# One Trainium2 core, a hybrid decoder layer: the recurrence's block-diagonal gate products on the two halves of the array's rows

## The chip, the core and the metric

The kernel runs as one program on one core of a Trainium2 chip. The metric is the device time of one execution in microseconds, the median of several runs. TensorE (PE) multiplies, ACT and DVE work on vectors of up to 128 partitions, POOL (GpSimd) takes some vector work, and SP issues the transfers.

## The reference, cut to what matters

One decoder layer on 16 meta tokens and 1024 tokens of width 1024 (T = 1040 positions): a norm, one wide projection, three mixers side by side (windowed attention, attention with forgetting, a recurrence), their gated sum, an output projection, then a gated feed-forward part and a last norm. The change is in the third mixer, the recurrence, whose 512 channels stand in 8 blocks of 64:

```python
xb = x.reshape(b, t, LRU_BLOCKS, LRU_BLOCK_DIM)              # 8 blocks of 64 channels
r = sigmoid(einsum('bthi,hij->bthj', xb, w_r) + b_r)         # each block has its own 64x64 weights
gi = sigmoid(einsum('bthi,hij->bthj', xb, w_i) + b_i)
log_a = LRU_C * r * log_sigmoid(lam)
h_t = exp(log_a) * h_{t-1} + sqrt(1 - exp(2 * log_a)) * gi * x
```

## The kernel before

All matmuls are exact to float32 by parts: an operand is split into a high part (hi) and a rest (lo), and a product is three matmuls, hi·hi, hi·lo and lo·hi (`mm3`, line 157, its matmul on line 164). `split` (line 128) makes the parts, the high one with ACT (line 131), the rest with DVE (line 132). PSUM has banks of 128x512 under four names: three `mm`, two `sc`, two `tr`, one `ob`. The order of the instructions on each engine is fixed when the program is built, by a scheduler that goes by readiness and by the order in which they were written; `keep_in_program_order` pins an instruction behind the one written before it on its engine. At run time each engine goes through its list in order.

The layer's stages follow each other: norm and first projections (to about 70 us), the recurrence together with the value projections (about 76 to 211 us on PE), attention together with the remaining projections and the branch gates, the branch sum, output projection, feed-forward. In the second of these, `drive` (line 253) mixes two generators: the main one, `lru_main` (line 569), yields projections, and the side one, `lru_side` (line 558), advances one step for each 3500 ns (`LRU_GAP`) of the main one's matmuls. A `yield None` in the side one is such a step. When the main one has nothing left, the side one runs on without it, and the scheduler may place the next stage's projections (gates, queries, keys) between.

The recurrence takes its 512 channels in four tiles m of 128, so two blocks of 64 stand in one tile, on partitions 0 to 63 and 64 to 127. The gate weights come as one array `w_bd` of 128 x 1024: for each tile and gate a 128x128 matrix with the two 64x64 blocks on its diagonal and zeros elsewhere. `lru` (line 508) does one tile: a width-4 convolution on DVE (lines 517, 519) gives x; `split` gives xh and xl; the second input's activation (lines 525 to 528); then for each of the two gates r and g, and each of the column stretches 0:272, 272:528 and 528:1040, one product of three matmuls into an `sc` bank and one sigmoid on ACT out of it (line 536); then tanh, exp and square root on ACT (lines 540, 541, 544), products, the scan and the output's product on DVE (lines 542, 545, 546, 549, 550), another split, and two transfers to DRAM. The gate's bias is one column of `part`, a tile of all small parameters, loaded from `par` at 19 us.

Of the kernel before, what the change touches and what calls it, by code (L numbers as in the profile page):

```python
# [9 lines left out]
F32 = mybir.dt.float32  # L10
F32R = mybir.dt.float32r
AF = mybir.ActivationFunctionType
# [4 lines left out]
P = 128  # L17
D = 1024
# [18 lines left out]
P_CW, P_CB, P_BR, P_BI, P_LM, P_NF = 0, 16, 20, 24, 28, 32  # L37
# [9 lines left out]
def f32(ap):  # L47
    return ap.bitcast(F32)
# [17 lines left out]
def hybrid_block(ctx, tc, h_in, w_in, w_v0, w_v1, w_bd, par, rows, gains, relt, onehot,  # L66
                 maskrow, cmask, w_br, w_out, w_fi, w_fo, out):
    nc = tc.nc
    act, dve, pool, pe = nc.scalar, nc.vector, nc.gpsimd, nc.tensor

    def dma(dst, src):
        nc.sync.dma_start(f32(dst) if dst.dtype == F32R else dst, f32(src) if src.dtype == F32R else src)

    def pad(pool, n):

        pool.tile([P, n // 4], F32, name=f"pad{uid[0]}")
        uid[0] += 1
# [3 lines left out]
    wp = ctx.enter_context(tc.tile_pool(name="wstream", bufs=2, side="left"))  # L81
# [11 lines left out]
    def nm(s):  # L93
        uid[0] += 1
        return f"{s}_{uid[0]}"

    def bank(tag, bufs, label):
        return pp.tile([P, 512], F32, tag=tag, bufs=bufs, name=nm(tag + label))

    mm_bank = lambda label="": bank("mm", 3, label)  # L100
    sc_bank = lambda label="": bank("sc", 2, label)
    tr_bank = lambda label="": bank("tr", 2, label)
# [25 lines left out]
    def split(hi, lo, src, scale=None, pin=False):  # L128

        if scale is None:  # L130
            a = act.activation(hi, src, AF.Copy)  # L131
            i = dve.tensor_tensor(lo, src, f32(hi), ALU.subtract)  # L132
            if pin:
                tc.keep_in_program_order(i)
        else:
            a = act.activation(hi, src, AF.Copy, scale=scale)
            i = dve.scalar_tensor_tensor(lo, src, scale, f32(hi), ALU.mult, ALU.subtract)
        return a.ins, i.ins

    def load_w(src, n, pl=None, tag="w", bufs=None, lo_on_pool=False):  # L140
        pl = pl or wp
        kw = {} if bufs is None else dict(bufs=bufs)
        if n == D:
            raw = wp.tile([P, n], F32, tag="wr", name=nm("wr"))
        else:
            raw = pl.tile([P, n], F32, tag=tag + "r", name=nm(tag + "r"), **kw)
        dma(raw, src)
        hi = pl.tile([P, n], F32R, tag=tag + "h", name=nm(tag + "h"), **kw)
        lo = pl.tile([P, n], F32R, tag=tag + "l", name=nm(tag + "l"), **kw)
        if lo_on_pool:  # L150
            act.activation(hi, raw, AF.Copy)
            pool.tensor_tensor(lo, raw, f32(hi), ALU.subtract)
        else:
            split(hi, lo, raw)
        return hi, lo

    def mm3(ps, terms, first=True):

        n = 3 * len(terms)
        cost = ps.shape[-1] / 2.4 + 3  # L160
        i = 0
        for ah, al, bh, bl in terms:
            for a, b in ((ah, bh), (ah, bl), (al, bh)):
                pe.matmul(ps, a, b, start=first and i == 0, stop=i == n - 1, skip_group_check=not first)  # L164
                i += 1
            yield 3 * cost

    def run(gen):
        for _ in gen:
            pass  # L170

    def log_sigmoid(dst, z, pl, shape):

        e, s, s2, a = (pl.tile(shape, F32, name=nm("ls")) for _ in range(4))
        dve.scalar_tensor_tensor(e, z, -1.0, z, ALU.mult, ALU.min)
        act.activation(e, e, AF.Exp)
        dve.tensor_scalar(s, e, 2.0, None, ALU.add)
        dve.reciprocal(s, s)
        dve.tensor_tensor(s, s, e, ALU.mult)
        dve.tensor_tensor(s2, s, s, ALU.mult)  # L180
        dve.tensor_scalar(a, s2, 1.0 / 17, 1.0 / 15, ALU.mult, ALU.add)
        for c in (13, 11, 9, 7, 5, 3, 1):
            dve.tensor_tensor(a, a, s2, ALU.mult)
            dve.tensor_scalar(a, a, 1.0 / c, None, ALU.add)
        dve.tensor_tensor(a, a, s, ALU.mult)
        dve.tensor_scalar(s, z, 0.0, None, ALU.min)
        dve.scalar_tensor_tensor(dst, a, -2.0, s, ALU.mult, ALU.add)
# [14 lines left out]
    def rstd_of(x, n, junk):  # L202

        q = cp.tile([P, 2], F32, tag="sq2", bufs=4, name=nm("sq"))
        for i in range(2):
            act.activation(junk[i], x[i], AF.Square, accum_out=q[:n, i:i + 1])
        return rstd_from(q, n)

    def halves(x):
        return x[:, :512], x[:, 512:]  # L210
# [80 lines left out]
    with tc.tile_pool(name="r0", bufs=1, side="right", reuse_waits="tile") as r0:  # L291
# [128 lines left out]
        def products(j, w, chunk):  # L420

            c, off, n, t0 = chunk
            ps = mm_bank(f"_w{j}")
            kinds = {"hh": (w[0], uh[c]), "hl": (w[0], ul[c]), "lh": (w[1], uh[c])}

            def some(kind, ks, first=False, last=False):
                a, b = kinds[kind]
                for k in ks:
                    t_.matmul(ps[:, :n], a[:, k * P:(k + 1) * P], b[:, k, off:off + n],
                              start=first and k == ks[0], stop=last and k == ks[-1])  # L430
            return ps[:, :n], some
# [33 lines left out]
        ps, some = products(YC, wy[0], (0, NM, 256, 0))  # L465
# [39 lines left out]

    r1 = ctx1.enter_context(tc.tile_pool(name="r1", bufs=1, side="right", reuse_waits="tile"))

    def lru(m, bdh, bdl):
        xr, y = lru_in[m]
        pc = lambda b: part[:, b + m:b + m + 1]  # L510
        cw = lambda i: part[:, P_CW + 4 * m + i:P_CW + 4 * m + i + 1]

        def t1(tag, dt=F32):
            return r1.tile([P, T], dt, tag=tag, bufs=1, name=nm(tag))

        x = t1("x")
        dve.tensor_scalar(x, xr[:, 0:T], cw(0), pc(P_CB), ALU.mult, ALU.add)
        for i in range(1, 4):
            dve.scalar_tensor_tensor(x, xr[:, i:i + T], cw(i), x, ALU.mult, ALU.add)
        xh, xl = t1("xh", F32R), t1("xl", F32R)  # L520
        split(xh, xl, x)
        yield None

        th = t1("th")[:, :S]
        act.activation(th, y, AF.Square, scale=math.sqrt(0.044715))
        dve.scalar_tensor_tensor(th, th, 1.0, y, ALU.add, ALU.mult)
        act.activation(th, th, AF.Tanh, scale=math.sqrt(2.0 / math.pi))
        dve.scalar_tensor_tensor(y, th, 1.0, y, ALU.add, ALU.mult)
        yield None
        r, g = t1("r"), t1("g")  # L530
        for dst, gi, b in ((r, 0, P_BR), (g, 1, P_BI)):
            col = slice((2 * m + gi) * P, (2 * m + gi + 1) * P)
            for t0, n in ((0, 272), (272, 256), (528, 512)):
                ps = sc_bank()
                run(mm3(ps[:, :n], [(bdh[:, col], bdl[:, col], xh[:, t0:t0 + n], xl[:, t0:t0 + n])]))
                act.activation(dst[:, t0:t0 + n], ps[:, :n], AF.Sigmoid, bias=pc(b))
                yield None

        w = t1("q")
        act.activation(w, r, AF.Tanh, scale=lsc[:, 0, m:m + 1])  # L540
        act.activation(r, r, AF.Exp, scale=lsc[:, 1, m:m + 1])
        dve.tensor_tensor(g, g, x, ALU.mult)
        yield None
        act.activation(w, w, AF.Sqrt)
        dve.scalar_tensor_tensor(w, r, 1.0, w, ALU.add, ALU.mult)
        dve.tensor_tensor(g, w, g, ALU.mult)
        yield None
        hs = t1("x")
        dve.tensor_tensor_scan(hs, r, g, 0.0, ALU.mult, ALU.add)
        dve.scalar_tensor_tensor(y, hs[:, NM:T], 0.5, y, ALU.mult, ALU.mult)  # L550
        yield None
        ch, cl = t1("xh", F32R), t1("xl", F32R)
        split(ch[:, :S], cl[:, :S], y)
        dma(osp[2, 0, m], ch[:, :S])
        dma(osp[2, 1, m], cl[:, :S])
        yield None

    def lru_side():
        bdh, bdl = load_w(w_bd, D, r1, "bd")
        pad(r1, 448)  # L560

        log_sigmoid(lsc[:, 1], part[:, P_LM:P_LM + 4], r1, [P, 4])
        dve.tensor_scalar(lsc[:, 0], lsc[:, 1], -4.0, None, ALU.mult)
        dve.tensor_scalar(lsc[:, 1], lsc[:, 1], 8.0, None, ALU.mult)
        for m in range(4):
            yield ("lru", m)
            yield from lru(m, bdh, bdl)

    def lru_main():
        done.update({("lru", 0), ("lru", 1)})  # L570
# [450 lines left out]
    with tc.tile_pool(name="r4", bufs=1, side="right", reuse_waits="tile") as r4:  # L1021
        with tc.tile_pool(name="r4b", bufs=1, side="right", reuse_waits="tile") as r4b:
            for c in range(2):
                u2[c] = [pair_tile(mp if c else bp) for k in range(KT // 2)]
                for tt in range(4 * c, 4 * c + 4):
                    ht = r4.tile([P, D], F32, tag="ht", bufs=2, name=nm("ht"))
                    dma(ht, h_in[NM + tt * P:NM + (tt + 1) * P])
                    t0 = (tt - 4 * c) * P
                    q = slice(t0, t0 + P)
                    for half in range(2):  # L1030
                        n = slice(512 * half, 512 * half + 512)
                        ps = mm_bank(f"_wo{tt}")
# [5 lines left out]
                    r = rstd_of(halves(ht), P, halves(xg))  # L1038
# [410 lines left out]
```

## Time and profile before

| | |
|---|---|
| median of 3 runs | 1641.56 us (1641.25 to 1641.89) |
| the profiled execution's own time | 1640.56 us |
| its span, first to last instruction | 1638.8 us |
| PE busy | 1627.0 us, 8189 matmuls |
| ACT, DVE, POOL busy | 760.5, 997.5, 388.3 us |

The profile is of one execution. Engine busy times are a union of the recorded instructions; a matmul's record includes its way through the array, so records of consecutive matmuls overlap, and the time that one costs is read from start to start. PEld are the weight loads of PE, recorded apart.

### The profile page before, as it was taken

How to read it: one execution, taken by the hardware profiler on the slowest of the kernel's cores; microseconds unless marked ns; L12 is line 12 of the kernel's file. 1: busy time of each engine (PE TensorE's matmuls, PEld its weight loads, DVE VectorE, ACT ScalarE, POOL GpSimd, SP SyncE). 2: the span in 40 equal slices, each digit the busy share in tenths (PEclk: the TensorE clock that was granted, in tenths of full speed). 3: DMA queues.
4: the chain of work that ended last, by engine and by line, in shares of the span. 5: the costliest groups of instructions: out<-in, count | busy, mean ns of one | idle time of the engine just before them, and what ended most of it. 6: DMA issues, size and time to landing. Idle time of an engine off the chain costs nothing.

```text
span 1638.8 us, 22729 instructions
## 1 busy us (share of the span) xinstructions
PE 1627.0 (99%) x8189; PEld 1373.6 (84%) x8189; DVE 997.5 (61%) x1817; ACT 760.5 (46%) x1399; POOL 388.3 (24%) x325
## 2 busy tenths in 40 slices
PE   9999999999999999999999999999999999999998
PEld 8898888888888888888888888888888888888886
DVE  6566666555666666642447447967777766466554
ACT  6456465555555555552335334433333333355342
POOL 3000000012122221110055000267756666200000
PEclk9999999999999999999999999999999999999999
DMA  6323342213324142349753322345554453698632
GB/s 224 110 95 104 120 139 97 94 64 123 117 78 123 59 124 82 106 138 332 259 183 116 119 88 76 126 159 181 212 178 148 154 182 114 224 352 277 195 127 103
DMA packets 110738, 241.96 MB, mean 148 GB/s; under 512 B 11929, under 2 KB 23529, under 8 KB 110370
## 3 DMA queue, kind: packets, MB, share of 16 engines
q1 hardware_dynamic: 110482, 239.99, 43.4%
q8 instruction: 64, 1.05, 0.3%
q10 hardware_dynamic: 144, 0.52, 0.1%
q14 instruction: 48, 0.39, 0.1%
HBM read 162.93 MB, written 72.21 MB: 143 GB/s over the span
## 4 chain that ended last, share of the span: by engine, by line
PE 93%; DVE 2%; ACT 2%; DMA 1%; issue 1%; SPq 0%; POOL 0%; DVEq 0%; ACTq 0%; POOLq 0%
PE mm_w L164 26%; PE mm_s L164 13%; PE mm_br L164 8%; PE tr_s L164 7%; PE mm_wo L164 5%; PE mm_x L1313 4%; PE tr_y L1313 4%; PE sc_y L1313 4%; PE mm_v L164 3%; PE sc_s L164 3%; PE ob L711 3%; PE tr L722 3%; PE ob_x L1313 1%; PE mm_g L164 1%; PE mm_u L164 1%; PE sc L796 1%
## 5 line engine op out<-in xcount | busy, mean ns | idle before, releaser
L164 PE MATMUL mm_w<-uh,wh 128*128 128x512 f32 (+2 forms) x744 | 291.5, 392 | 0.0
L164 PE MATMUL mm_w<-uh,wl 128*128 128x512 f32 (+2 forms) x744 | 279.4, 376 | 0.0
L164 PE MATMUL mm_w<-ul,wh 128*128 128x512 f32 (+2 forms) x744 | 279.4, 375 | 0.0
L164 PEld LDWEIGHTS mm_w<-uh,wl 128*128 128x128 f32 x744 | 140.0, 188 | 25.3
L164 PEld LDWEIGHTS mm_w<-uh,wh 128*128 128x128 f32 x744 | 140.4, 189 | 12.5
L164 PEld LDWEIGHTS mm_w<-ul,wh 128*128 128x128 f32 x744 | 140.8, 189 | 11.5
L132 DVE TENSOR_TENSOR ab<-raw,ab 128x1024 fp32r<-128x1024 f32 x77 | 92.8, 1223 | 72.0 <-ACT ab L131 71.5
L131 ACT ACTIVATE ab<-raw 128x1024 fp32r<-128x1024 f32 x77 | 80.8, 1060 | 95.3 <-PE ob_x L1313 23.3
L131 ACT ACTIVATE wh<-wr 128x1024 fp32r<-128x1024 f32 (+1 forms) x84 | 72.0, 859 | 106.8 <-PE mm_w L164 50.5
L164 PE MATMUL mm_br<-o,wh 128*128 128x512 f32 x384 | 118.3, 389 | 0.0
L164 PE MATMUL mm_s<-pt,ar 128*128 128x512 f32 x492 | 118.2, 389 | 0.0
L132 DVE TENSOR_TENSOR pl<-tr,ph 128x384 fp32r<-128x384 f32 (+2 forms) x160 | 87.2, 554 | 47.1 <-ACT ph L131 43.0
L164 PEld LDWEIGHTS mm_s<-pt,ar 128*128 128x128 f32 x492 | 92.3, 188 | 19.2
L132 DVE TENSOR_TENSOR wl<-wr,wh 128x1024 fp32r<-128x1024 f32 x45 | 56.7, 1261 | 72.0 <-ACT wh L131 71.8
L131 ACT ACTIVATE ph<-tr 128x384 fp32r<-128x384 f32 (+2 forms) x160 | 76.9, 486 | 50.3 <-PE tr L722 48.2
L812 POOL TENSOR_SCALAR s<-s,sm 128x144 f32<-128x144 f32 (+3 forms) x64 | 48.6, 761 | 171.8 <-DVE sm L811 143.4
L164 PE MATMUL mm_wo<-wo,hl 128*128 128x512 f32 x384 | 89.2, 391 | 0.0
L164 PEld LDWEIGHTS mm_br<-o,wh 128*128 128x128 f32 x384 | 72.1, 188 | 15.0
L164 PEld LDWEIGHTS mm_wo<-wo,hl 128*128 128x128 f32 x384 | 71.6, 188 | 14.7
L722 PE MATMUL tr<-ident,s 128*128 128x128 f32 x480 | 79.8, 274 | 0.8 <-DVE pl L132 0.2
L164 PE MATMUL mm_br<-o,wl 128*128 128x512 f32 x192 | 74.7, 389 | 0.0
L722 PEld LDWEIGHTS tr<-ident,s 128*128 128x128 f32 x480 | 59.0, 140 | 18.0 <-DVE pl L132 3.9
(315 smaller groups left out, 3580.7 us busy)
## 6 DMA issues: line engine op xcount, KB each, us to landing
wr<-w_in_dram SPq DMA_DIRECT2D x45, 512.0 KB, 3.6
wr<-w_fi_dram SPq DMA_DIRECT2D x44, 512.0 KB, 4.5
raw<-asp SPq DMA_DIRECT2D x77, 256.0 KB, 3.3
asp<-a SPq DMA_DIRECT2D x66, 256.0 KB, 2.8
gz<-z SPq DMA_DIRECT2D x48, 256.0 KB, 2.1
sg<-gz SPq DMA_DIRECT2D x48, 256.0 KB, 2.7
o<-osp SPq DMA_DIRECT2D x24, 512.0 KB, 4.9
fo<-w_fo_dram SPq DMA_DIRECT2D x22, 512.0 KB, 4.4
```

The source lines that it names most:

```text
L131: a = act.activation(hi, src, AF.Copy)
L132: i = dve.tensor_tensor(lo, src, f32(hi), ALU.subtract)
L164: pe.matmul(ps, a, b, start=first and i == 0, stop=i == n - 1, skip_group_check=not first)
L711: pe.matmul(ob[:, q0:q0 + b - a], vt[:, c], x[:, a:b], start=count == 0, stop=count == n_mm - 1, skip_group_check=True)
L722: pe.transpose(tb[:, col:col + P], src, ident)
L796: pe.matmul(sc[:, :n], qs, kh[:, k0:k0 + n], start=True, stop=False)
L812: pool.tensor_scalar(s[:, :nk], s[:, :nk], den, 1.0, ALU.mult, ALU.mult)
L1313: pe.matmul(banks[x], a[:, 0, q], b[:, 1], start=first and j == 0 and c == 0, stop=j == NJ - 1 and c % 3 == 2, skip_group_check=True)
```

## The change

The gate products no longer multiply by a 128x128 matrix with two zero blocks. The weights are rearranged: rows 0 to 63 hold, for each tile, the first block's 64 columns of gate r and then of gate g, rows 64 to 127 the same of the second block, so that the array `bdh` (and `bdl`) is 128 x 512, and a half of it, 64 rows by 128 columns, is both gates of one block. For each column stretch there are two banks, one from `sc` and one from `tr`. Three products (hi·hi, hi·lo, lo·hi) are written, each as a matmul of rows 0 to 63 into the first bank and one of rows 64 to 127 into the second; all but the first of the six are pinned behind the matmul written before. A bank then holds gate r of its block in partitions 0 to 63 and gate g in 64 to 127, so four activations of 64 partitions take the two banks apart. They need their biases by bank partitions: a new tile `bias2` is filled by four small transfers from `par`. The two `split` calls of the weights go over 64 rows each. The padding behind shrinks by as much as `bias2` takes.

```diff
-    def lru(m, bdh, bdl):
+    def lru(m, bdh, bdl, bias2):
...
-        for dst, gi, b in ((r, 0, P_BR), (g, 1, P_BI)):
-            col = slice((2 * m + gi) * P, (2 * m + gi + 1) * P)
-            for t0, n in ((0, 272), (272, 256), (528, 512)):
-                ps = sc_bank()
-                run(mm3(ps[:, :n], [(bdh[:, col], bdl[:, col], xh[:, t0:t0 + n], xl[:, t0:t0 + n])]))
-                act.activation(dst[:, t0:t0 + n], ps[:, :n], AF.Sigmoid, bias=pc(b))
+        for t0, n in ((0, 272), (272, 256), (528, 512)):
+            sl = slice(t0, t0 + n)
+            banks = sc_bank()[:, :n], tr_bank()[:, :n]
+            for i, (a, b) in enumerate(((bdh, xh), (bdh, xl), (bdl, xh))):
+
+                for z, ps in enumerate(banks):
+                    rw = slice(64 * z, 64 * z + 64)
+                    mm = pe.matmul(ps, a[rw, m * P:m * P + P], b[rw, sl], start=i == 0, stop=i == 2)
+                    if i or z:
+                        tc.keep_in_program_order(mm)
+            for z, ps in enumerate(banks):
+                rw = slice(64 * z, 64 * z + 64)
+                for gi, dst in enumerate((r, g)):
+                    src = slice(64 * gi, 64 * gi + 64)
+                    act.activation(dst[rw, sl], ps[src], AF.Sigmoid, bias=bias2[src, z, m:m + 1])
                 yield None
...
-        bdh, bdl = load_w(w_bd, D, r1, "bd")
-        pad(r1, 448)
+        raw = wp.tile([P, D], F32, tag="wr", name=nm("wr"))
+        dma(raw, w_bd)
+        raw = raw.rearrange("p (m g c) -> p m g c", m=4, g=2)
+        bdh, bdl = (r1.tile([P, D], F32R, tag=f"bd{x}", name=nm(f"bd{x}"))[:, :512] for x in "hl")
+
+        bias2 = r1.tile([P, 2, 4], F32, name="bias2")
+        for z in range(2):
+            rw = slice(64 * z, 64 * z + 64)
+            split(*(x[rw].rearrange("p (m g c) -> p m g c", m=4, g=2) for x in (bdh, bdl)), raw[rw, :, :, rw])
+            for gi, b in enumerate((P_BR, P_BI)):
+                dma(bias2[64 * gi:64 * gi + 64, z], par[rw, b:b + 4])
+        pad(r1, 416)
...
-            yield from lru(m, bdh, bdl)
+            yield from lru(m, bdh, bdl, bias2)
```

## Rows read from the trace of the kernel before

**Rows 1.** The page's head: span, busy time of each engine, the granted clock in 40 slices (9 is full speed within a tenth), and the chain of work that ended last, by engine.
```profile
span 1638.8 us, 22729 instructions
PE 1627.0 (99%) x8189; PEld 1373.6 (84%) x8189; DVE 997.5 (61%) x1817; ACT 760.5 (46%) x1399; POOL 388.3 (24%) x325
...
PEclk9999999999999999999999999999999999999999
...
PE 93%; DVE 2%; ACT 2%; DMA 1%; issue 1%; SPq 0%; POOL 0%; DVEq 0%; ACTq 0%; POOLq 0%
```

**Rows 2.** Busy time of each engine in the recurrence's stage (stretch, its length, then PE, PEld, DVE, ACT, POOL with their instructions, the granted clock, the DMA engines' share and GB/s): the whole stretch, 15 us near its end, and the whole stretch for the instructions of the `sc` banks alone.
```profile
75.00:211.00 136.00, 134.81 (x806) 122.31 (x805) 81.06 (x138) 78.61 (x108) 0.00 (x0) 1.00 0.32 111
...
195.00:210.00 15.00, 13.81 (x80) 11.90 (x79) 11.12 (x13) 8.78 (x14) 0.00 (x0) 1.00 0.47 148
...
75.00:211.00 136.00, 15.12 (x72) 11.75 (x72) 0.00 (x0) 12.09 (x24) 1.00 0.32 111
```

**Rows 3.** What PE waited for between 60 and 330 us: engine, tile and line, the releaser, the total in us, how often, the longest.
```profile
PE sc L164 <- ACT xh L131: 1.2, 1, 1.2
```

**Rows 4.** The timeline around one gate product of each column stretch (start and duration in us, engine, line, operation, out<-in, rows*columns of the weights, the moving operand): PE, and for the first group PE's weight loads.
```profile
76.54 0.29 PE L164 MATMUL sc<-xh,bdh 128*128 128x272 f32 x1
76.92 0.39 PE L164 MATMUL mm_w<-uh,wh 128*128 128x512 f32 x1
...
76.55 0.19 PEld L164 LDWEIGHTS sc<-xl,bdh 128*128 128x128 f32 x1
...
81.02 0.28 PE L164 MATMUL sc<-xh,bdh 128*128 128x256 f32 x1
81.38 0.39 PE L164 MATMUL mm_w<-uh,wh 128*128 128x512 f32 x1
...
84.78 0.39 PE L164 MATMUL sc<-xh,bdh 128*128 128x512 f32 x1
85.47 0.39 PE L164 MATMUL mm_w<-uh,wh 128*128 128x512 f32 x1
```

**Rows 5.** The timeline around the one product of 32 rows (two matmuls, merged into one line in the first view; the line that begins at 30.95 is the second of them, from a view that begins there), and the weight load of the 32-row product.
```profile
30.30 0.28 PE L164 MATMUL mm_w<-ul,x1h 128*128 128x256 f32 x1
30.41 0.28 PE L164 MATMUL mm_w<-uh,x1l 128*128 128x256 f32 x1
30.62 0.81 PE L482 MATMUL sc<-oh,rt 32*8 32x383 f32 x2
...
30.62 0.09 PEld L482 LDWEIGHTS sc<-oh,rt 32*8 32x8 f32 x2
...
30.95 0.48 PE L482 MATMUL sc<-oh,rt 32*8 32x383 f32 x1
31.36 0.66 PE L218 MATMUL tr<-ident,xg 128*128 128x128 f32 x4
```

**Rows 6.** The timeline where gate products stand between small transposes whose weights have 8 columns: PE, then one weight load of such a transpose.
```profile
148.26 0.48 PE L164 MATMUL sc<-xh,bdh 128*128 128x512 f32 x1
148.57 0.27 PE L592 MATMUL tr<-ident,lf 128*8 128x128 f32 x1
148.60 0.48 PE L164 MATMUL sc<-xl,bdh 128*128 128x512 f32 x1
...
148.37 0.08 PEld L592 LDWEIGHTS tr<-ident,lf 128*8 128x8 f32 x1
```

**Rows 7.** ACT's groups of instructions by shape, 55 to 235 us: out<-in, shapes, count, busy us, mean ns, idle before.
```profile
L536 ACT ACTIVATE r<-sc,part 128x512 f32<-128x512 f32 x4 | 2.8, 689 | 5.2 <-PE sc L164 5.2
L536 ACT ACTIVATE r<-sc,part 128x272 f32<-128x272 f32 x4 | 2.0, 489 | 0.3 <-PE sc L164 0.3
...
L536 ACT ACTIVATE g<-sc,part 128x256 f32<-128x256 f32 x4 | 1.9, 474 | 0.0
...
L283 ACT ACTIVATE xr<-mm_w 128x512 f32<-128x512 f32 x3 | 1.8, 586 | 4.8 <-PE mm_w L164 4.8
...
L131 ACT ACTIVATE k<-mm_w 64x512 fp32r<-64x512 f32 x2 | 1.2, 594 | 0.1
```

**Rows 8.** The chain of work that ended last, in order of time (start, us, what): its stretch through the recurrence's third tile to the operand of the fourth, and the end of the attention stage.
```profile
181.46 1.05 ACT q L540
...
202.27 1.08 ACT xh L131
...
729.00 42.85 PE mm_w L164 x189
```

**Rows 9.** The timeline where the gate weights are split, and the issues of SP's queue (SPq) beside it: the small parameters' transfer, and the load that follows the split.
```profile
19.14 0.42 SPq L72 DMA_DIRECT2D part<-par_dram  x1
...
55.66 1.05 ACT L131 ACTIVATE bdh<-wr 128x1024 fp32r<-128x1024 f32 x1
...
57.99 0.33 SPq L72 DMA_DIRECT2D wr<-w_in_dram  x1
...
66.29 1.05 ACT L131 ACTIVATE wh<-wr 128x1024 fp32r<-128x1024 f32 x1
```

**Rows 10.** The weight loads of a run of attention products, of which two have only 128 columns.
```profile
706.24 0.19 PEld L711 LDWEIGHTS ob<-pl,v 128*128 128x128 f32 x1
706.35 0.19 PEld L711 LDWEIGHTS ob<-ph,v 128*128 128x128 f32 x1
706.46 0.19 PEld L711 LDWEIGHTS ob<-pl,v 128*128 128x128 f32 x1
```

## The prediction, on record before the changed kernel ran

> **What bounds the kernel now.** I read the page's head first, then the chain that ended last, then the recurrence's stretch alone. TensorE is busy in 1627.0 of 1638.8 us, at a granted clock of full speed (the 2.4 GHz level) in all 40 slices [rows 1]; the chain is 93% PE [rows 1]. So time taken out of TensorE's order of work is time off the end, as long as nothing new makes it wait. The change lies between 76 and 211 us. There TensorE is busy in 134.8 of 136 us and ACT in 78.6; what TensorE lacks lies at 195 to 210 [rows 2]. PE waited for the recurrence once, 1.2 us, for the operand of the last channel tile [rows 3].
>
> **The products' own time.** One gate product is three matmuls. Start to start, from a group's first matmul to the next tile's first, a group of 272 columns takes 76.92 - 76.54 = 0.38 us, one of 256 columns 81.38 - 81.02 = 0.36, one of 512 columns 85.47 - 84.78 = 0.69 [rows 4]. Weight loads begin as the matmul ahead begins, and so are hidden [rows 4]. Four channel tiles with two gates make 8 x (0.38 + 0.36 + 0.69) = 11.4 us of TensorE. That is all the change can touch: 0.7% of the run. (By one row for all 72, the stretch's busy time in these banks is 15.1 us, but a matmul's record reaches over the start of the next [rows 2].)
>
> **Part 1, half the rows, two at a time.** The new loop has as many matmuls and as many columns: per column stretch three products times two halves, against three times two gates. It gains only if the matmul on rows 64 to 127 runs while that on rows 0 to 63 runs. Nothing in this trace has two matmuls on different rows at once, so the bounds are: below, each pair takes the time of one, 4 x 1.43 = 5.7 us in place of 11.4 (a gain of 5.7); above, they run one after the other, 11.4 again. I take the lower figure: the two have no weight, row or bank in common, and the engine does start a matmul of 8 columns and the next of 128 within 0.03 us of each other (148.57 and 148.60) [rows 6].
>
> **Part 2, going into half rows and out again.** The trace has one place where TensorE goes from all rows to a part of them and back, a product of 32 rows at 30.62 us. The matmul ahead begins at 30.41 and, of 256 columns, takes 0.12 as its forerunners do, so it is through at 30.53; the 32-row one begins at 30.62, and its weights are loaded then, not under the matmul ahead: 0.09 us lost [rows 5]. On the way back, the second begins at 30.95, takes 0.33 like the first (30.95 - 30.62), is through at 31.28; the next full one begins at 31.36 with its load: 0.08 lost [rows 5]. A load that is not hidden holds up its own matmul too: the gate products between transposes last 0.48 instead of 0.39 us, 0.09 more [rows 4, 6]. So one visit costs 0.09 + 0.09 + 0.08 + 0.09 = 0.35 us. The new loop makes at most 12 visits (4 tiles x 3 stretches, other work between them): 4.2 us. Bounds: 0, if 64 rows are no change of state for the array as 32 were; 4.2 above. I take 4.2, since these are the only rows with such a step. The Trainium skill (TensorEngine Tiling, Key Properties) says that a change of tiling mode drains the engine; by that rule the sum is the one below, without it the gain would be the whole 5.7 us. The trace agrees for 32 rows, and has no row for 64.
>
> **Part 3, sigmoids.** 24 activations of 128 rows become 48 of 64 rows, with as many columns each. Halving the rows saves nothing: a 64x512 copy takes 594 ns, a 128x512 one 586 [rows 7]. So ACT gets 8 x (0.49 + 0.48 + 0.69) = 13.3 us more [rows 7], over 136 us in which it is busy for 78.6 [rows 2]. For tiles 0 and 1 the main stream's products cover it. For tiles 2 and 3 the products come in a burst and the rest hangs in a chain of ACT and DVE work from 180 to 203 us, at the end of which PE waited [rows 3, 8]; the chain gets about 3.3 us longer per tile. Taken at 0: 42.85 us of one TensorE run, four gate projections with nothing beside them, stand behind the attention stage at 729 us, and such work can be ordered ahead while the recurrence lags [rows 8]. Without that cover it costs up to 2 x 3.3 = 6.6 us.
>
> **Part 4, banks, the split and the small transfers.** The second half takes transpose banks, of which there are two, as of the others; a column stretch now holds its two banks for four activations, some 2 us, and the next stretch has the other two: 0, bounded by one such wait, 2 us. Five of the six matmuls are pinned in their written order, which adds no wait. Splitting the weights on 64 rows twice instead of 1024 columns once: ACT 1.05 us becomes 2 x 0.59 [rows 7, 9], and DVE's part is taken to grow alike. The weight buffer comes free about 0.2 us later for the load that SP issues at 57.99, needed at 66.29 [rows 9]: hidden. Four transfers into the new bias tile join SP's queue; an issue like theirs takes 0.42 us [rows 9], so 1.7 us, and SP has nothing to issue for many us before 57.99. If they were to stand behind a buffer that is late, the load at 57.99 would be late with them, against a slack of some 4 us. Cost 0, above 2 us, nothing to gain.
>
> **The sum.** -11.4 + 5.7 + 4.2 = -1.5 us. The profiled execution took 1640.56 us, of which 1638.8 are the span; it lies 1.0 below the median of the runs, 1641.56. From the median: 1640.1 us, 0.1% down. A measurement here can tell apart about 0.2%, 3.3 us; so the forecast is no difference that shows.
>
> **Rivals.**
> Whole gain: the halves overlap and the visits are nearly free, because 64 rows with loads for each half let the next load run ahead. Then 1641.6 - 5.7 = 1635.9 us, or about 1637 with half of the 0.17 us of a visit's two gaps. For it: at 148.37 the weights of an 8-column transpose are loaded under a full matmul [rows 6]. Against: the 32-row load was not [rows 5].
>
> Weight loads set the pace: loads of 128 columns come no closer than 0.11 us (706.24, 706.35, 706.46) [rows 10], and a pair needs two. In turn, a pair takes 0.22, 0.22 and 0.23 us, 12 x 0.67 = 8.0 with three products and four tiles; -11.4 + 8.0 + 4.2 = +0.8: 1642.4 us. If a half's load also waited for that half's own matmul, a pair would be its columns' time plus 0.11: 12 x (0.125 + 0.12 + 0.23 + 0.33) = 9.7, and the sum is +2.5, 1644.1 us. The Trainium skill (TensorE: Matmul & The Clock Gate, Part 3, The mechanism) has loads overlap running matmuls only where the row groups differ, which is this last case. The trace speaks against the rule: on all rows a load begins at 76.55 beside a matmul of the same rows that began at 76.54 [rows 4].
>
> **Slower:** the change doesn't do what it says, the halves run one after the other. Then the visits are all that is left: +4.2, 1645.8 us, slower by 0.26%. It decides from the first pair: starts of the two halves a full 0.12 or 0.23 us apart. For it: no row of two matmuls running whole side by side; against: nothing that they share.
>
> Late recurrence: the chain of tiles 2 and 3 ends 6.6 us later and TensorE's order has its products too early; -1.5 + 6.6 = +5.1, 1646.7 us. For it: the 1.2 us wait that is there now [rows 3]; against: the spare gate work.
>
> **Chances.** Forecast 0.42, whole gain 0.24, weight loads 0.14, one after the other 0.11, late recurrence 0.09. Faster by over 0.2% (under 1638.3) is the whole gain and the edge of the forecast: 0.25. Slower (over 1644.8) is the last two and an edge of the weight loads: 0.22. Within: 0.53. The range goes from just under the whole gain, 1635.5, to 1645.3, which leaves out the last rival and most of the one before it. The forecast's own range is 1638 to 1642.
>
> **What would show it.** Starts of the halves of a pair within 0.11 us of each other and pairs 0.12 or 0.23 apart: part 1 right. A gap of about 0.09 ahead of the first half-row matmul, its load not under the matmul ahead, and the same on the way out: part 2 right. Pairs 0.22 apart whatever their columns: the weight loads. ACT's busy time up by 13 us with PE's waits for xh unchanged: part 3 right. I am wrong if PE's total falls by 5 us or more, or if PE waits for sigmoids or banks.

## The result and the profile after

The changed kernel took 1649.71 us (median of 6 runs, 1647.54 to 1654.34), the kernel before 1641.71 beside it: ratio 1.005, interval 1.0039 to 1.006. That is 8 us or 0.5% slower, outside the range of the prediction and on the side that had a chance of 0.22. The profiled execution is the quickest of the six, 1647.54 us, with a span of 1645.7 against 1638.8 before: 6.9 us to explain. The three longest runs (1650.7 to 1654.3 us) have a mean granted clock of 0.996, the three shortest 0.998 or 0.999, so the time spent at the lower clock differs between executions of the same program.

The head of the page after: span, busy times, and TensorE's busy tenths in 40 slices.

```profile
span 1645.7 us, 22757 instructions
PE 1629.6 (99%) x8189; PEld 1369.5 (83%) x8189; DVE 1003.7 (61%) x1818; ACT 772.7 (47%) x1422; POOL 390.8 (24%) x325
PE   9999989999999999999999999999999999999998
```

Beside [rows 1] there are as many matmuls, ACT has 12.2 us more, and one slice of TensorE, the sixth (206 to 247 us), shows an 8. What TensorE waited for between 60 and 330 us (releaser, total, times, longest; two waits of 0.3 us are left out):

```profile
PE sc L768 <- DVE sm L770: 2.2, 1, 2.2
PE sc L538 <- ACT g L545: 1.5, 1, 1.5
PE mm_w L164 <- DVE wl L132: 1.2, 1, 1.2
PE sc L538 <- ACT xh L131: 0.8, 1, 0.8
```

Before, there was 1.2 for xh [rows 3]. Now xh has 0.8, and three new waits of over 1 us stand beside it. Busy time by stretch (PE, PEld, DVE, ACT, POOL, the granted clock, DMA share, GB/s): one stretch after, then the sums from 60 to 330 us, after and before:

```profile
180.00:195.00 15.00, 13.74 (x53) 10.51 (x54) 3.17 (x3) 13.33 (x19) 0.00 (x0) 0.89 0.09 37
...
sum 270.00, PE 263.34 PEld 224.42 DVE 165.34 ACT 165.40 POOL 9.88; mean PE 14.63 PEld 12.47 DVE 9.19 ACT 9.19 POOL 0.55
...
sum 270.00, PE 268.06 PEld 234.52 DVE 169.92 ACT 158.45 POOL 9.98; mean PE 14.89 PEld 13.03 DVE 9.44 ACT 8.80 POOL 0.55
```

The 15 us from 180 had a mean clock of 0.89, so 15 x 0.11 = 1.65 us of TensorE's work was lost there. Over 60 to 330 us, TensorE's idle time is 270 - 263.34 = 6.66 us against 1.94 before. Idle 4.7 and clock 1.65 make 6.4 us. The products themselves give back about 1.0 (below), so 7.9 us are to be explained and 1.5 are in neither sum. An idle time begins only where the record of the matmul ahead ends: the wait that shows 1.46 us below is 181.26 - 179.29 = 1.97 us from start to start, less 0.34 for the matmul ahead (0.23, and 0.11 for its load, as below) 1.63. At 0.17 us more for each of six waits, an estimate, that is 1 of the 1.5 us; the last 0.5 stay open.

**The products themselves came out as forecast.** PE at the first gate group (start, duration, line, out<-in, rows*columns of the weights, moving operand), then PE's loads for the second pair:

```profile
76.36 0.39 PE L164 MATMUL mm_w<-uh,wl 128*128 128x512 f32 x1
76.68 0.39 PE L538 MATMUL sc<-xh,bdh 64*128 64x272 f32 x1
76.68 0.39 PE L538 MATMUL tr<-xh,bdh 64*128 64x272 f32 x1
76.91 0.29 PE L538 MATMUL sc<-xl,bdh 64*128 64x272 f32 x1
76.91 0.29 PE L538 MATMUL tr<-xl,bdh 64*128 64x272 f32 x1
77.04 0.28 PE L538 MATMUL sc<-xh,bdl 64*128 64x272 f32 x1
77.04 0.28 PE L538 MATMUL tr<-xh,bdl 64*128 64x272 f32 x1
77.25 0.50 PE L164 MATMUL mm_w<-uh,wh 128*128 128x512 f32 x1
```
```profile
76.79 0.19 PEld L538 LDWEIGHTS sc<-xl,bdh 64*128 64x128 f32 x1
76.79 0.19 PEld L538 LDWEIGHTS tr<-xl,bdh 64*128 64x128 f32 x1
```

Both halves of each pair begin at the same hundredth. From the first pair to the next full matmul it is 77.25 - 76.68 = 0.57 us, with 0.09 ahead of it (76.36, and 0.23 as its like take, to 76.68), and the full matmul behind is 0.11 longer than its like (0.50 against 0.39): 0.77 in all, where two gate groups took 2 x 0.38 [rows 4].

**Where the time went.** ACT at channel tile 2, from the table load ahead of its sigmoids to the tanh and the table load behind that:

```profile
178.93 1.28 ACT L545 ACT_TABLE_LOAD   x1
180.23 0.48 ACT L545 ACTIVATE r<-sc,bias 64x272 f32<-64x272 f32 x1
180.72 0.48 ACT L545 ACTIVATE g<-sc,bias 64x272 f32<-64x272 f32 x1
...
186.99 1.17 ACT L549 ACTIVATE q<-r,lsc 128x1040 f32<-128x1040 f32 x1
188.17 1.28 ACT L550 ACT_TABLE_LOAD   x1
```

and PE beside it:

```profile
179.29 0.51 PE L164 MATMUL mm_w<-uh,wh 128*128 128x512 f32 x1
181.26 0.50 PE L538 MATMUL sc<-xh,bdh 64*128 64x512 f32 x1 [1.46 <-ACT g L545]
...
184.07 0.63 PE L164 MATMUL mm_w<-uh,wl 128*128 128x512 f32 x1
184.50 0.63 PE L164 MATMUL mm_w<-uh,wh 128*128 128x512 f32 x1
...
187.24 0.39 PE L164 MATMUL mm_w<-ul,wh 128*128 128x512 f32 x1
187.47 0.40 PE L164 MATMUL mm_w<-uh,wl 128*128 128x512 f32 x1
```

The two pairs of banks are full, and the third stretch waits until ACT has loaded its table and read the first bank twice. Then matmuls of 512 columns stand 0.43 us apart (184.07, 184.50) where they take 0.23 at 187.24 and 187.47: the 1.2 GHz level, from about 183.5 to 186.9. The tanh begins at 186.99; before, it began at 181.46 by the chain [rows 8]. That compares unlike places: the old order had gate r complete after its own three sigmoids, and two of gate g's stood behind the tanh; now r is complete only with the last stretch. All sigmoids of the tile are done where ACT loads the table behind them; before, its first sigmoids and that load:

```profile
178.85 0.85 ACT L536 ACTIVATE r<-sc,part 128x272 f32<-128x272 f32 x2
...
183.48 1.28 ACT L541 ACT_TABLE_LOAD   x1
```

So the tile is 188.17 - 183.48 = 4.7 us late there. From ACT's first sigmoid (180.23 after, 178.85 before) it is 7.94 against 4.63 us: 3.3 us are the added sigmoids, and the rest is mostly the table load at 178.93, which ACT did not have at that place before.

The end of tile 3 (DVE: the split of x, before and after, and the last product y, before and after; then SP's queue, then DVE in the next stage, after):

```profile
203.37 1.24 DVE L132 TENSOR_TENSOR xl<-x,xh 128x1040 fp32r<-128x1040 f32 x1 [0.74 <-ACT xh L131]
208.38 1.24 DVE L132 TENSOR_TENSOR xl<-x,xh 128x1040 fp32r<-128x1040 f32 x1 [0.72 <-ACT xh L131]
223.54 1.23 DVE L550 SCALAR_TENSOR_TENSOR y<-x,y 128x1024 f32<-128x1024 f32 x1
232.78 1.23 DVE L559 SCALAR_TENSOR_TENSOR y<-x,y 128x1024 f32<-128x1024 f32 x1
233.92 1.22 DVE L132 TENSOR_TENSOR wl<-wr,wh 128x1024 fp32r<-128x1024 f32 x1
...
245.92 0.37 DVE L770 CUSTOM_DVE_ANT_0 s<-sc,nb,nsink 128x144 f32<-128x144 f32 x1 [4.09 <-DMA nb<-bss]
```
```profile
235.12 0.32 SPq L72 DMA_DIRECT2D osp<-xh  x1
...
239.69 0.89 SPq L72 DMA_DIRECT2D nb<-bss  x2
```

DVE splits the next stage's weights (wl) only behind the recurrence's last product y: PE waits 1.2. SP issues the attention's bias `nb` behind the recurrence's last store `osp`: DVE's softmax step waits for it, its bank stays taken, and PE waits 2.2. Both are places in a fixed list behind an instruction that has become late: before, SP issued `osp` at 225.88 and `nb` at 230.55, about as far apart.

### The profile page after: what moved, and what is told of

The parts are those of the page before. It is cut to its first block, busy times and chain, and to the rows that moved or that the text cites. A ratio compares the mean times of both kernels' runs of the same rounds, so it can differ in the third digit from the quotient of the medians.

```text
span 1645.7 us, 22757 instructions
## 1 busy us (share of the span) xinstructions
PE 1629.6 (99%) x8189; PEld 1369.5 (83%) x8189; DVE 1003.7 (61%) x1818; ACT 772.7 (47%) x1422; POOL 390.8 (24%) x325
## 4 chain that ended last, share of the span: by engine, by line
PE 93%; ACT 3%; DVE 2%; DMA 1%; issue 1%; SPq 0%; POOL 0%; DVEq 0%; ACTq 0%; POOLq 0%
PE mm_w L164 25%; PE mm_s L164 13%; PE mm_br L164 8%; PE tr_s L164 7%; PE mm_wo L164 5%; PE mm_x L1333 4%; PE tr_y L1333 4%; PE sc_y L1333 4%; PE ob L731 4%; PE mm_v L164 3%; PE sc_s L164 3%; PE tr L742 3%; PE ob_x L1333 1%; PE mm_g L164 1%; PE mm_u L164 1%; PE sc L816 1%
```

## The experiments

Theories: **A**, the doubled sigmoids lengthen ACT's part of the recurrence's chain, and what stands behind it in the queues is late. **B**, the half-row products and their pairs of banks cost by themselves. **C** (later called **L**), no price but another order: the scheduler places everything differently, and a fixed order meets banks and operands that are not ready. **P**, the pace of the recurrence's steps; **T** and **S** belong to e13, **E** to e14 and e15. Differences below are in us against the kernel before in its own runs; at 1640 us the intervals reach 1.5 to 2.5 us to either side.

**e1.** The kernel before, with each sigmoid in two halves.

```diff
-                act.activation(dst[:, t0:t0 + n], ps[:, :n], AF.Sigmoid, bias=pc(b))
+                for z in range(2):
+                    rw = slice(64 * z, 64 * z + 64)
+                    act.activation(dst[rw, t0:t0 + n], ps[rw, :n], AF.Sigmoid, bias=pc(b)[rw])
```


> The kernel before with its 128x128 products, but each of the 24 sigmoids taken in two halves of 64 rows, so ACT has the changed kernel's 48 sigmoids and PE the old work. Theory A (the loss is ACT's: the doubled sigmoids make tiles 2 and 3 of the recurrence late and hold banks): 4 to 8 us above the kernel before, y of the last tile (DVE, the product after the scan) at about 230 us instead of 223.5, and PE waits for nb or wl near 235 to 245 us. Theory B (the loss is in the half-row products: visits, their clock): within 1 us of the kernel before. Theory C (any edit here that makes the scheduler order the work anew costs this much): a shift of either size, with the waits at other places than in the changed kernel.

1647.54 us, +6.1. The last y begins at 231.24, and PE waits 1.9 for xh and 1.3 for the attention's `sm`. At this pace, the sigmoids alone cost nearly what the change costs.

**e2.** Half-row products, but one sigmoid of 128 rows per bank.

```diff
-                rw = slice(64 * z, 64 * z + 64)
-                for gi, dst in enumerate((r, g)):
-                    src = slice(64 * gi, 64 * gi + 64)
-                    act.activation(dst[rw, sl], ps[src], AF.Sigmoid, bias=bias2[src, z, m:m + 1])
+                act.activation((r, g)[z][:, sl], ps, AF.Sigmoid, bias=bias2[:, z, m:m + 1])
```


> The changed kernel's half-row products, but one sigmoid of 128 rows for each bank (24 in all, as before), written whole into r or g. What is left out: the rearrangement of the gates by block, so r and g hold mixed rows and the output is not the reference's. Theory A: the loss is gone, 1.5 us below the kernel before to 1 us above it, the recurrence's last y at about 222 to 224 us. Theory B: still 6 to 8 us above. Theory C: anything, with waits at new places.

1648.86 us, +7.1, so the products alone also cost nearly the whole: A by itself is not enough, or one order tells little. What PE waited for:

```profile
PE mm_w L164 <- DVE q L673: 5.2, 2, 4.3
PE sc L538 <- ACT r L542: 1.4, 1, 1.4
```

The 5.2 us are evictions of the next stage's queries, which DVE had among the recurrence's last products, up to behind y (219.30 to 227.0 us); stretches at the lower clock follow both waits (180 to 195 us: 1.65 us, 225 to 240: 3.0). The last y begins at 225.08, only 1.5 us late: at this pace most of the loss came without a late end.

**e3.** The third stretch in other banks.

```diff
-            banks = sc_bank()[:, :n], tr_bank()[:, :n]
+            banks = (sc_bank(), tr_bank()) if t0 < 528 else (o_bank(), mm_bank())
+            banks = [x[:, :n] for x in banks]
```


> The changed kernel, with the 512-column stretch's two banks taken from ob and mm instead of sc and tr, so the third stretch need not wait for the sigmoids of the first. Theory A with its bank part: PE's wait of 1.5 us at 181 us and the stretch at the lower clock behind it (1.7 us) go, 2 to 4 us below the changed kernel, so 3 to 6 above the kernel before; the late end of the recurrence and its waits near 235 to 245 us stay. If the bank wait is not a cause: as the changed kernel.

1666.48 us, +25: one wait of 26.1 us at 180. As the kernel reads, the `mm` banks go round in written order, so the next stage's projections had to wait for tile 3's product; no run tests this. The experiment says nothing about bank holding.

**e4 to e8 and e18.** Old and changed kernel at other paces, which give other orders.

```diff
-LRU_GAP = 3500.0
+LRU_GAP = 2500.0   # e4, e18; 3000.0 in e5, e6; 4000.0 in e7, e8
```


> The changed kernel with the recurrence's steps spaced 2500 instead of 3500 ns of main work. Theory A: the recurrence runs further ahead beside the value projections, its last y comes 5 us or more earlier than 232.8, and 3 to 7 us of the loss go (within 4 us of the kernel before). Theory B: as the changed kernel, 6 to 8 us above. Theory C: anything.

> The kernel before with LRU_GAP 3000 in place of 3500: the side generator is advanced every 3000 ns of the main one's matmuls, so the recurrence's work is put earlier among the projections; products and sigmoids as before. Theory L (the change's own price is small; any other order of the work between 178 and 260 us meets banks and operands that are not ready, and the kernel before at 3500 happens to be a well-timed order): slower than before, by 2 to 8 us, with waits of PE of over 1 us in that stretch. Theory A (the added sigmoids themselves make the recurrence late, whatever the order): without the added sigmoids no loss, 1639 to 1643.

> The changed kernel with LRU_GAP 3000. Theory L: its difference to the old products at the same gap lies anywhere from -4 to +4 us. Theory A: +4 to +8 us above the old products at the same gap.

> The kernel before with LRU_GAP 4000: the recurrence's work is put later among the projections. Theory L: slower than before by 2 to 8 us, with waits of PE of over 1 us between 178 and 260 us. Theory A: a later recurrence alone costs some too, but less than the changed kernel loses: 1641 to 1645.

> The changed kernel with LRU_GAP 4000. Theory L: its difference to the old products at the same gap lies anywhere from -4 to +4 us. Theory A: +4 to +10 us above the old products at the same gap, since the recurrence starts later still.

> The kernel before at LRU_GAP 2500, where the changed kernel took 1646.03 us. Theory A: 1639 to 1643, the changed kernel 3 to 7 us above. If the changed kernel's loss were gone at this early pace, 1644 or above.

With e16 and e17 (below), each median with its ratio to the kernel before:

| LRU_GAP | old products | half rows, whole sigmoids | changed |
|---|---|---|---|
| 2500 | 1641.69, 1.0005 | | 1646.03, 1.0029 |
| 3000 | 1643.49, 1.0014 | 1645.64, 1.0024 | 1655.03, 1.0081 |
| 3500 | 1641.71 (the kernel before) | 1648.86, 1.0043 | 1649.71, 1.005 |
| 4000 | 1641.19, 0.9996 | 1642.37, 1.0005 | 1648.74, 1.0041 |

The old products lose 2 us or less at every pace, so another pace alone does not make the loss. L is not out as a part of it: in e14, one more order, the old products lose 5.3 us. The changed kernel stands above them by 3.9, 11.0, 8.2 and 7.4 us (from the differences of the ratios, each good to some 2 to 3 us): the change costs at each of four orders. The size goes with the order: 4 to 11 us. A's ranges were missed three times: e6 is above its 4 to 8 us, e4, 4.8 us above the kernel before, is just over its 4, and e5 is 0.5 us above its 1643.

**e9 and e10.** The change also drops steps of the side generator, from twelve per tile to nine, which the prediction had not counted. e9 gives the changed kernel its six gate steps back, e10 takes three from the kernel before.

```diff
                     act.activation(dst[rw, sl], ps[src], AF.Sigmoid, bias=bias2[src, z, m:m + 1])
-                yield None
+                    if gi:
+                        yield None
```
```diff
                 act.activation(dst[:, t0:t0 + n], ps[:, :n], AF.Sigmoid, bias=pc(b))
-                yield None
+                if (gi, t0) in ((0, 272), (1, 0), (1, 528)):
+                    yield None
```


> The changed kernel with six steps of the side generator per tile in the gate part, as the kernel before has (a yield after each bank's two sigmoids, in place of one per column stretch). Before makes 12 steps per tile, the change 9, so that at one step per 3500 ns its recurrence is written denser among the projections. Theory P (the missing steps make the recurrence's products and sigmoids come in bursts for which banks and ACT are not ready): 1640 to 1643. Theory A (the doubled sigmoids make it late whatever the pace): 1646 to 1650. Theory L (order by luck): anything from 1641 to 1652.

> The kernel before with three steps per tile in place of six in the gate part (two products and two sigmoids per step); products and sigmoids as before. Theory P: slower than before by 5 to 9 us, since the pace alone does it. Theory A: no loss, 1640 to 1643.

1648.26 (+6.6) and 1643.47 us (+1.5, interval 0.9999 to 1.0018). The pace is not it: P falls. (e10 is 0.5 us above A's range.)

**e11.** The change in tiles 0 and 1 alone.

```diff
+        if m in (0, 1):
...
+        else:
+            for dst, gi, b in ((r, 0, P_BR), (g, 1, P_BI)):
```


> The change for channel tiles 0 and 1 alone; tiles 2 and 3 keep the products on 128 rows, six sigmoids of 128 rows and six steps. If the loss arises where the last two tiles' chain hangs on ACT (theory A, and P as well): 1640.5 to 1643, no loss. If half-row products cost something by themselves in each tile: 1643 to 1646. Theory L: 1641 to 1650.

1643.06 us, +1.3 (0.9999 to 1.0018). That is on the border of the first two ranges (1643). In this order nearly the whole loss goes with tiles 2 and 3, whose products stand behind the last value projection (its last matmul begins at 178.1 us before and after). Sigmoids and half-row products were taken out of them together, so the run does not tell which of the two it is.

**e12.** No table loads inside the recurrence's chain.

```diff
-        act.activation(w, r, AF.Tanh, scale=lsc[:, 0, m:m + 1])
-        act.activation(r, r, AF.Exp, scale=lsc[:, 1, m:m + 1])
+        act.activation(w, r, AF.Sigmoid, scale=lsc[:, 0, m:m + 1])
+        act.activation(r, r, AF.Sigmoid, scale=lsc[:, 1, m:m + 1])
...
-        act.activation(w, w, AF.Sqrt)
+        act.activation(w, w, AF.Sigmoid)
```


> The changed kernel with the recurrence's tanh, exp and square root all replaced by sigmoids of the same shape (the output is not the reference's), so that ACT loads no other function's table between a tile's sigmoids and its scan: two loads of 1.28 us fewer per tile, three where the sigmoids' own load goes too, against 3.3 us that the added sigmoids take. Theory A: the last y comes about as early as in the kernel before, and the loss falls to 0 to 3 us: 1641 to 1645. Theory P: the bursts stay: 1646 to 1650.

1648.06 us, +6.4: A's number is missed. The bank wait at 179 fell to 0.3 us, with the load ahead of it gone, and the last y begins at 225.94, not 232.78. But PE waits 2.4 us for xh of tile 3, from 202.0, and the clock goes down behind that wait:

```profile
195.00:210.00 15.00, 12.62 (x65) 9.37 (x64) 10.21 (x12) 6.36 (x12) 0.00 (x0) 0.81 0.34 122
210.00:225.00 15.00, 15.00 (x58) 11.41 (x59) 7.93 (x7) 10.86 (x17) 0.00 (x0) 0.85 0.33 72
```

15 x 0.19 + 15 x 0.15 = 5.1 us are the clock's. What A had as its price, a late end, shrank, and the loss did not; a stretch at the 1.2 GHz level is most of it.

**e13.** The changed kernel with the sigmoid's table loaded early.

```diff
         split(xh, xl, x)
+        act.activation(warm, f32(xh[:, 0:1]), AF.Sigmoid)
```


> The changed kernel with one sigmoid of a single column behind each tile's split of x, so that ACT's table for sigmoids is loaded while the products wait for their operand, and not in front of the first sigmoid that has to free a bank. In the changed kernel this load (1.28 us, at 178.93) stands ahead of tile 2's sigmoids, TensorE waits 1.46 us for their bank at 179.8 to 181.26, and a stretch at the lower clock follows (15 us at a mean of 0.89: 1.65 us). Theory T (that is 3 us of the loss of 8; what follows later is the recurrence's late end, by itself worth 3 to 5): 1644 to 1647. Theory S (the late end hangs on this wait too): 1640 to 1643. Theory L: no gain, 1647 to 1651.

1647.34 us, +6.2 (1.0023 to 1.0053), just above T's range, inside L's, and not apart from the changed kernel. ACT and, below, PE's two largest waits:

```profile
174.72 1.28 ACT L522 ACT_TABLE_LOAD   x1
```
```profile
PE sc L770 <- DVE sm L772: 3.1, 2, 3.0
PE sc L539 <- ACT xh L131: 2.5, 1, 2.5
```

The bank wait fell from 1.5 to 0.3 us and the clock stayed at 1.00 from 180 to 195. Up to 205 us PE was busy for 202.6 us, against 202.2 in the kernel before, and then it gave all of that back: the wait for tile 3's xh grew from 0.8 to 2.5, that behind `nb` from 2.2 to 3.0, and both have a stretch at the lower clock behind them (210 to 225: 1.5 us, 240 to 255: 1.65). So this wait has no price of its own that shows: in this trace PE runs ahead of a late chain (last y at 231.80) and waits where it next meets it. The trace is of the longest of e13's four runs (1649.2 us), that of the changed kernel of the quickest of six, so sizes of single waits are not to be compared closely.

**e14 and e15.** Both kernels with tile 3's projections ahead of the value projections.

```diff
+        yield from proj(XC + 3, FULL, xs)
+        yield from proj(YC + 3, REAL, ys)
+        done.add(("lru", 3))
         yield from values(1, w_v1, 328)
...
-        yield from proj(XC + 3, FULL, xs)
-        yield from proj(YC + 3, REAL, ys)
-        done.add(("lru", 3))
```


> The kernel before with the projections of the last channel tile written ahead of the value projections of the second half instead of behind them, so that tile 3 can begin some 45 us earlier and the recurrence ends beside projections. Theory E (what the change costs is a late end of the recurrence that meets the next stage): 1638 to 1643, hardly any difference here, since the end is not what this kernel waits for.

> The changed kernel with the same reordering. Theory E: the late end is gone, and with it the waits between 230 and 250 us; within 2 us of the old products in the same order (1637 to 1644). Theory B (the change costs wherever it stands): 5 to 9 us above the old products in the same order.

1646.68 (+5.3) and 1652.16 us (+11.5). The reordering did not do what it was for: tile 3 still begins late (its xl at 209.79 and 216.06 us), 9.4 and 9.7 us behind the y of the tile before it (200.36, 206.36), as it does elsewhere: that tile sets its start, not its input. Theory E stays untried by it. As a fifth order it has the changed kernel 6.2 us above the old products (by the ratios; 5.5 by the medians), as theory B has it.

**e16 and e17.** e2's edit at the paces 3000 and 4000.

> Half-row products with six whole sigmoids of 128 rows per tile (the gates are mixed, so the output is not the reference's) at LRU_GAP 3000. At this pace the old products took 1643.49 and the changed kernel 1655.03 us. Theory A (the loss is the added time of ACT in the chain of tiles 2 and 3; the 7.6 us that the products alone lost at 3500 were one unlucky order): -2 to +3 us against the old products, 1641 to 1646.5. Theory B (the half-row products and their two banks lose by themselves): +5 us or more, 1648 or above.

> The same at LRU_GAP 4000, where the old products took 1641.19 and the changed kernel 1648.74 us. Theory A: 1639 to 1644. Theory B: 1646 or above.

1645.64 and 1642.37 us, 1.6 and 1.5 above the old products at the same pace, which is not clear of the noise and within A's ranges. Putting the doubled sigmoids on top costs 9.4 and 5.9 us more (1655.03 and 1648.74). So at two paces of three the products by themselves neither lose much nor gain, and the doubled sigmoids are the loss; at 3500 the products lose 7.1, and the sigmoids on top only 1.1. That e2's loss was for the most part an order is the likeliest reading, not shown. Tile 3 at the pace 4000 (DVE: start of the split of x, start of the last product y), for the old products (e7), half rows with whole sigmoids (e17) and the change (e8):

```profile
203.19 1.24 DVE L132 TENSOR_TENSOR xl<-x,xh 128x1040 fp32r<-128x1040 f32 x1 [0.74 <-ACT xh L131]
223.35 1.23 DVE L550 SCALAR_TENSOR_TENSOR y<-x,y 128x1024 f32<-128x1024 f32 x1
```
```profile
205.79 1.24 DVE L132 TENSOR_TENSOR xl<-x,xh 128x1040 fp32r<-128x1040 f32 x1 [0.73 <-ACT xh L131]
225.14 1.23 DVE L556 SCALAR_TENSOR_TENSOR y<-x,y 128x1024 f32<-128x1024 f32 x1
```
```profile
202.61 1.23 DVE L559 SCALAR_TENSOR_TENSOR y<-x,y 128x1024 f32<-128x1024 f32 x1
214.12 1.23 DVE L132 TENSOR_TENSOR xl<-x,xh 128x1040 fp32r<-128x1040 f32 x1
236.90 1.22 DVE L559 SCALAR_TENSOR_TENSOR y<-x,y 128x1024 f32<-128x1024 f32 x1
```

From xl to y it is 20.2 us, 19.4 and 22.8. And the chain is one: tile 3 needs buffers that tile 2 leaves (there is one each of x, xh and xl), 11.5 us from tile 2's y (202.61) to tile 3's xl (214.12), 10.1 in e7 and 9.4 in e17, so a late tile 2 makes tile 3 late: the last y comes 13.5 us late in e8, 1.8 in e17. At all paces (start of the last y; TensorE's idle time from 60 to 330 us; what it lost there at the lower clock, from windows of 15 us; all in us):

| LRU_GAP | last y: old, half rows with whole sigmoids, changed | idle: old, changed | lower clock: old, changed |
|---|---|---|---|
| 2500 | 199.71, not run, 211.72 | 2.72, 6.16 | 0, 0 |
| 3000 | 219.08, 224.25, 229.74 | 2.72, 11.44 | 0, 5.1 |
| 3500 | 223.54, 225.08, 232.78 | 1.94, 6.66 | 0, 1.65 |
| 4000 | 223.35, 225.14, 236.90 | 1.92, 6.24 | 0, 0 |

The last y is 9 to 14 us late in the changed kernel at every pace and 7.7 in e1, against 1.5 to 5.2 with whole sigmoids: the doubled sigmoids make half of the lateness or more. That r is complete later, which e2, e16 and e17 have too, can be only a part of the rest. How much a late chain costs is not read from its end. At 2500 the changed kernel's last y stands 12 us ahead of that of the kernel before at 3500, and it still loses 3.9 us to the old products at its pace; it waits inside the recurrence there, 2.9 us for xh and 2.0 for `cum`. The lower clock is no needed part of the loss either: at 2500 and 4000 the change costs without it.

## Why the prediction was wrong, by its own steps

**Bound and part 1: right.** The halves of a pair start together and pairs follow by 0.12 to 0.13 us (76.91, 77.04). The Trainium skill (TensorE: Matmul & The Clock Gate, Part 3, The mechanism) has loads overlap running matmuls only where the row groups differ, by one line of that section; another there lets them run ahead into a background weight buffer too. Here the loads for both halves begin at 76.79, beside both halves' running matmuls, so the trace goes on speaking against the first line and fits the second. The rival of the weight loads, with its pairs 0.22 apart, falls by the pairs' starts.

**Part 2: right, a little small.** A visit costs 0.09 going in, 0.11 for its own load, 0.10 going out (77.04 and 0.11 for 272 columns, to 77.25) and 0.11 for the next load: 0.41 against 0.35. The Trainium skill (TensorEngine Tiling, Key Properties) says that a change of tiling mode drains the engine; with 64 rows too the trace agrees, by 0.09 and 0.10 us. By the same reading a group of 256 columns takes 0.75 us in place of 2 x 0.36, and one of 512, from 93.34 to 94.24 with 0.09 ahead and 0.11 behind, 1.10 in place of 2 x 0.69. With 0.77 against 0.76 for 272 that is -0.24 us per tile, -1 in all, against -1.5 forecast.

**Part 3: the size about right, the step that follows wrong.** ACT got 12.2 us more (13.3 forecast), and tile 3's chain grew by 22.8 - 20.2 = 2.6 us at the pace 4000 and by 24.4 - 20.2 = 4.2 at 3500, where 3.3 were forecast. Wrong is "taken at 0": spare gate products would be ordered ahead while the recurrence lags. The order is fixed when the program is built, and they were not placed ahead. The same 189 matmuls stand in one run behind the attention stage, 7.1 us later than at 729.00 [rows 8]; the chain that ended last, after:

```profile
736.07 42.88 PE mm_w L164 x189
```

What lay behind the late chain in the queues of DVE, ACT and SP was the next stage's weights, evictions and bias, and PE met those late: 4.7 us more idle and 1.65 at the lower clock, in place of 0. The late recurrence was a rival, at 1646.7 and with a chance of 0.09. The wait at the end of that chain [rows 3] spoke for it, and e1, the table of paces, and e17 against e8 point to it; e2 and e12 don't, whose last y is only 1.5 and 2.4 us late and which lose 7.1 and 6.4 us. So at 3500 a late chain is what the trace shows ahead of the waits, and how much of the 8.2 us is its own is not shown. The rival was too small as well: it counted two tiles at 3.3 us, but the last y came 9.2 us late at 3500 (232.78 against 223.54). It was 3.3 late after tile 1 (163.43 against 160.09), which was to be covered, and 5.7 after tile 2 (198.95 against 193.25).

**Part 4: the bound held, its consequence was missed.** The bank wait came once, 1.5 us of the 2 allowed, and behind it a stretch at the 1.2 GHz level of 1.65 us, which no term held. In e13 that wait was taken away, and nothing clear of the noise was gained. The split (ACT 2 x 0.63 us) and the small transfers cost nothing that shows.

**The sign that was to tell.** "ACT up by 13 us with PE's waits for xh unchanged" came true, 12.2 and 0.8 against 1.2, and part 3 was wrong all the same: it watched one wait where the lateness could come out in any queue. The other sign, waits for sigmoids or banks, did tell.

**Open.** Why each half of the change alone, at 3500, costs nearly as much as both (6.1 and 7.1 of 8.2). What sets how the loss at one pace splits between late operands and lower clock: in e12 and e13 the one took the place of the other. And whether a recurrence that ends beside projections would free the change of its price: e14 and e15 did not bring one about, and e4, the earliest end of the changed kernel, lost 3.9 us.

## What to carry to other kernels

Time added to an engine that is half idle is not free where a serial chain goes through it: measure one turn of the chain from its first to its last instruction, multiply the added time by the turns that nothing separates, and look at what stands behind its last instruction in every queue, SP's included. Cover counts only if it stands at that place in the fixed order. Where an edit changes the order, one build says little: run old and new at several paces and compare pairs.

## What the runs showed of the hardware

- Matmuls on rows 0 to 63 and 64 to 127, into two banks, begin and go on together, and so do their weight loads (76.68, 76.79). Going in and out again costs 0.41 us a visit, so with three pairs of 272 or 256 columns it eats the whole gain; at 512 columns it leaves 0.3 us of 1.38.
- Sixty-four rows cost ACT what 128 do: 481 to 485 ns against 489 for 272 columns.
- Waits of TensorE were followed by stretches at the 1.2 GHz level in some places (1.5 us in the changed kernel, 1.4 and 4.3 in e2, 2.4 in e12, 2.5 and 3.0 in e13) and not in others (2.2 in the changed kernel at 244, 2.0 and 1.5 in e4, 1.9 in e1, 1.7 and 1.5 in e8); in e12, e13 and the changed kernel such a stretch cost 1.5 to 5.1 us, from about half the wait ahead of it to twice that. What decides, these runs don't show.
